# A four-layer decoder trunk: compute order fixed by a clock of TensorE's work, q and k projected transposed, mixer and output projection in one stretch

## The chip, the core and the metric

The kernel runs as one program on one core of a Trainium2 chip. A core has TensorE (PE, matrix multiply), VectorE (DVE), ScalarE (ACT), GpSimd (POOL) and SyncE (SP, which here issues the DMAs). The metric is the device time of one execution in microseconds (us); lower is better. Three runs of the kernel before gave a median of 1271.38 us (1270.69 to 1271.77).

## The reference

Four layers over 256 tokens of 1024 features. Layer i uses mixer i mod 3, so the order is A, B, C, A. All is float32.

```python
for i in range(DEPTH):                      # DEPTH = 4
    kind, j = i % N_MIXERS, i // N_MIXERS
    if kind == 0:   h = mixer_a(...)        # window 128, 16 query heads, 4 key/value heads, sinks, biases
    elif kind == 1: h = mixer_b(...)        # 3 groups of q, k, v (dilation 1, 4, 16), merged by softmax sums
    else:           h = mixer_c(...)        # with 256 tokens: plain causal attention, 16 heads
    x = layer_norm(DN_ALPHA * x + h, ln_g[i, 0], ln_b[i, 0])
    x = layer_norm(DN_ALPHA * x + swiglu(x, w_gate_up[i], w_down[i]), ln_g[i, 1], ln_b[i, 1])
```

In each mixer q and k are projected (x @ w), then rotated on the first 16 of a head's 64 features: pairs (f, f+8) turn by an angle that depends on the token. Scores, softmax, values and an output projection follow. A, B and C have 3, 18 and 6 chunks of projection weights, and two chunks of output weights each; a chunk is 1024 x 512 weights.

## The kernel before

Every float32 product is made of three float16 products (`mm3`, L130 to L132): a weight chunk is scaled by 256 and split into `whi` and `wlo`, the activations into `xth` and `xtl`, and hi x hi, hi x lo and lo x hi are summed in PSUM. `load_w` brings a chunk in two DMAs of 1 MB into `raw`; ACT makes `whi` (L91) and DVE makes `wlo` (L92), 1024 columns at a time, four such pieces a chunk. `wlo` reads `raw` and `whi`, both in SBUF. Four chunks fit in the pool.

A projection (`proj`) takes 128 tokens as the stationary side and a chunk's 512 columns as the moving side, so q and k come out with tokens on the partitions. The bias (mixer A: DVE, L477) or the scaling (ACT, L543 for B and C) brings them to SBUF as `qkv`, POOL rotates them in four small operations (`rope`, L197 to L200, 64 or 128 columns), PE transposes four blocks of 128 x 128 (L206), and `split` writes `qkh` (ACT, L135) and `qkl` (DVE, L137). In mixer A, k is also copied twice over for its four query heads (L488).

`attend` writes out, for each item (a token tile and one or two pairs of heads): scores (L256), masked minimum on DVE (L266), exponential on ACT (L271), transposes of the weights (`flip`, L285), `ph` and `pl` (ACT, DVE), values into `pv` (L130 to L132), division (L309, L311), transposes of the output (L324), `oth` and `otl`. `weave` mixes these steps evenly with the projection steps of the next heads; the last heads are woven with the output projection in `finish`. This source order is only a priority: the framework's scheduler then orders each engine by its own estimate of readiness.

`layer_norm` adds the residual (L349), takes statistics (L351, L353), the root on POOL (L355) and scales (L358, L360, each with two SBUF inputs); then x is transposed (L160) for the next stage. In mixer A the output bias is added to x by DVE (L520, L522). The SwiGLU stage (`ffn`) projects with the weights as the stationary side and 256 tokens moving (128 for its first three chunks), then projects down.

At the start x comes first over SP, then the weights; PE begins with transposes of x.

Of the kernel before, what the change touches and what calls it, by code (L numbers as in the profile page):

```python
# [18 lines left out]
P = 128  # L19
# [24 lines left out]
def trunk(ctx, tc, a, out):  # L44
    nc = tc.nc
    pool = lambda name, bufs, **kw: ctx.enter_context(tc.tile_pool(name=name, bufs=bufs, **kw))
# [14 lines left out]
    cc = const.tile([P, NT, ROT], F32, name="cc")  # L61
    ss = const.tile([P, NT, ROT], F32, name="ss")
    h8 = ROT // 2
# [3 lines left out]
    X = []  # L67
    for t in range(NT):
        xt = const.tile([P, D], F32, name=f"x{t}")
        for h in range(2):  # L70
            nc.sync.dma_start(xt[:, h * 512:h * 512 + 512], a["x"][t * P:(t + 1) * P, h * 512:h * 512 + 512])
        X.append(xt)

# [3 lines left out]
    LAG, LF, LV, LO = 8, 1, 2, 3  # L77
    tok = lambda t: slice(t * P, (t + 1) * P)

    def load_w(src, n=8, piece=2048):  # L80

        hi = w_p.tile([P, 4096], F16, name="whi")
        lo = w_p.tile([P, 4096], F16, name="wlo")
        for c in range(0, n * 512, piece):
            m = min(piece, n * 512 - c)
            s = slice(c, c + m)
            r = raw_p.tile([P, 2048], F32, name="raw")
            nc.sync.dma_start(r[:, :m], src[:, s])
            for d in range(0, m, 1024):
                e = min(d + 1024, m)  # L90
                nc.scalar.activation(hi[:, c + d:c + e], r[:, d:e], AF.Copy, scale=WS)  # L91
                nc.vector.scalar_tensor_tensor(lo[:, c + d:c + e], r[:, d:e], WS, hi[:, c + d:c + e],  # L92
                                               op0=OP.mult, op1=OP.subtract)
        return (hi.rearrange("p (k n) -> p k n", n=512), lo.rearrange("p (k n) -> p k n", n=512))

    def weight_list():
        for li in range(DEPTH):
            kind, j = li % 3, li // 3
            if kind == 0:
                for c in (2, 0, 1):  # L100
                    yield a["w_a"][j, c], 8
# [14 lines left out]
    loaded = []  # L116

    def prefetch(n=1, piece=2048):
        for _ in range(n):
            loaded.append(load_w(*next(weights), piece))  # L120

    def next_w():
        if not loaded:
            prefetch()
        return loaded.pop(0)

    def mm3(ps, st, mv, start, stop):
# [4 lines left out]
        nc.tensor.matmul(ps, st[1], mv[0], start=False, stop=stop)  # L132

# [6 lines left out]

    def sl2(pair, *idx):
        return tuple(p.__getitem__(idx) for p in pair)

    def weave(main, fill):

        nf = 0
# [227 lines left out]
    def new_ps():  # L374
        return {}
# [366 lines left out]
```

## Time and profile before

| | us |
|---|---|
| median of three runs | 1271.38 |
| the profiled execution, whole | 1270.83 |
| its span, first to last instruction | 1268.3 |
| PE busy | 1238.2 |
| DVE busy | 868.7 |
| ACT busy | 657.4 |
| POOL busy | 126.2 |

The profiled execution stands within the three runs, 0.55 us under their median; 2.5 us of it lie outside the span. The granted clock of TensorE was 0.998 over the span. A matmul's record in the trace is longer than the distance to the next one, because matmuls overlap in the pipeline; so PE's busy time hides short waits, and what PE must do at least is read from the distance between the starts of neighbours.

### The profile page before, as it was taken

Reading aid. Unit: us, or ns where it says so; the run is one execution under the profiler, and the core shown is the slowest. Engines: PE = TensorE matmul, PEld = TensorE weight load, DVE = VectorE, ACT = ScalarE, POOL = GpSimd, SP = SyncE. Lnnn points to the kernel's source line nnn. Section 1 sums busy time; section 2 is a strip of 40 time slices with the busy share of each in tenths; the row PEclk is TensorE's granted clock in tenths of the full one; section 3 lists DMA queues with packets and bytes.
Section 4 is the critical chain, followed back from the end, with each engine's and each line's share of the span. In section 5 each row is a group of like instructions: output and inputs, shape, how many; then the busy total and the mean of one; then the engine's idle time right before and its main releaser. Section 6 shows DMA issues by size and latency. Waiting matters only on the chain. (4 is left out here: it accounts for less than half of the span.)

```text
span 1268.3 us, 24652 instructions
## 1 busy us (share of the span) xinstructions
PE 1238.2 (98%) x10352; PEld 829.0 (65%) x10352; DVE 868.7 (68%) x1431; ACT 657.4 (52%) x1097; POOL 126.2 (10%) x262
## 2 busy tenths in 40 slices
PE   7989999999999999999999999999999999999997
PEld 3549988445455555599884445599884445898843
DVE  5997766576576666777665766777665788776652
ACT  5855654345565655556543456556543465465430
POOL 2510000012121112000000110200000041000000
PEclk9999999999999999999999999999999999999999
DMA  8545755655444345147556564247555652475520
GB/s 322 175 164 200 267 201 185 218 206 216 167 163 170 133 147 186 67 168 266 199 183 207 208 217 149 100 167 267 199 183 206 230 186 101 168 266 200 182 84 34
DMA packets 35662, 233.30 MB, mean 184 GB/s; under 512 B 4448, under 2 KB 4448, under 8 KB 9696
## 3 DMA queue, kind: packets, MB, share of 16 engines
q1 hardware_dynamic: 35552, 231.74, 51.8%
q8 instruction: 81, 1.33, 0.4%
q14 instruction: 29, 0.24, 0.1%
HBM read 230.68 MB, written 1.05 MB: 183 GB/s over the span
## 5 line engine op out<-in xcount | busy, mean ns | idle before, releaser
L92 DVE SCALAR_TENSOR_TENSOR wlo<-raw,whi 128x1024 f16<-128x1024 f32 x416 | 501.4, 1225 | 207.2 <-ACT whi L91 206.6
L91 ACT ACTIVATE whi<-raw 128x1024 f16<-128x1024 f32 x416 | 414.5, 1049 | 260.0 <-PE acc L131 89.1
L131 PE MATMUL acc<-xtl,whi 128*128 128x256 f16 (+1 forms) x1792 | 408.2, 250 | 0.0
L132 PE MATMUL acc<-xth,wlo 128*128 128x256 f16 (+1 forms) x1792 | 408.2, 250 | 0.0
L130 PE MATMUL acc<-xth,whi 128*128 128x256 f16 (+1 forms) x1792 | 408.0, 250 | 0.0
L130 PE MATMUL acc<-whi,xth 128*128 128x512 f16 x480 | 183.3, 382 | 2.5 <-ACT xth L135 2.5
L130 PEld LDWEIGHTS <-whi 128*128 128x128 f16 x1792 | 175.3, 98 | 12.0
L131 PEld LDWEIGHTS <-whi 128*128 128x128 f16 x1792 | 175.3, 98 | 11.9
L131 PE MATMUL acc<-wlo,xth 128*128 128x512 f16 x480 | 183.0, 381 | 0.2 <-DVE wlo L92 0.2
L132 PE MATMUL acc<-whi,xtl 128*128 128x512 f16 x480 | 182.8, 381 | 0.3
L132 PEld LDWEIGHTS <-wlo 128*128 128x128 f16 x1792 | 175.3, 98 | 11.7
L130 PE MATMUL acc<-whi,hth 128*128 128x512 f16 x352 | 133.4, 379 | 0.0
L131 PE MATMUL acc<-wlo,hth 128*128 128x512 f16 x352 | 133.4, 379 | 0.0
L132 PE MATMUL acc<-whi,htl 128*128 128x512 f16 x352 | 133.4, 379 | 0.0
L355 POOL TENSOR_TENSOR mv<-mv,nhalf 128x1 f32<-128x1 f32 x16 | 15.8, 988 | 817.2 <-DVE mv L354 817.2
L132 PEld LDWEIGHTS <-xtl 128*128 128x128 f16 x480 | 47.1, 98 | 58.2 <-DVE xtl L137 3.0
L271 ACT ACTIVATE s<-s,mn 128x257 f32<-128x257 f32 (+5 forms) x128 | 66.8, 525 | 33.3 <-DVE mn L266 33.3
L130 PEld LDWEIGHTS <-xth 128*128 128x128 f16 x480 | 47.2, 98 | 48.9 <-issue 4.6
L135 ACT ACTIVATE hth<-hf 128x256 f16<-128x256 f32 x88 | 36.5, 415 | 73.7 <-DVE hf L399 73.7
L131 PEld LDWEIGHTS <-xth 128*128 128x128 f16 x480 | 47.2, 98 | 41.6 <-issue 0.8
L132 PEld LDWEIGHTS <-htl 128*128 128x128 f16 x352 | 34.4, 98 | 41.5
L131 PEld LDWEIGHTS <-hth 128*128 128x128 f16 x352 | 34.4, 98 | 40.8
(92 smaller groups left out, 1427.7 us busy)
## 6 DMA issues: line engine op xcount, KB each, us to landing
raw<-in_w_gu SPq DMA_DIRECT2D x88, 1024.0 KB, 5.0
raw<-in_w_dn SPq DMA_DIRECT2D x40, 1024.0 KB, 4.9
raw<-in_w_b SPq DMA_DIRECT2D x36, 1024.0 KB, 5.0
raw<-in_w_c SPq DMA_DIRECT2D x12, 1024.0 KB, 5.1
raw<-in_w_a SPq DMA_DIRECT2D x10, 1024.0 KB, 5.5
raw<-in_w_ao SPq DMA_DIRECT2D x8, 1024.0 KB, 5.5
gb<-in_ln_g SPq DMA_DIRECT2D x8, 512.0 KB, 4.7
gb<-in_ln_b SPq DMA_DIRECT2D x8, 512.0 KB, 6.2
```

What stands on the lines that cost most here:

```text
L91: nc.scalar.activation(hi[:, c + d:c + e], r[:, d:e], AF.Copy, scale=WS)
L92: nc.vector.scalar_tensor_tensor(lo[:, c + d:c + e], r[:, d:e], WS, hi[:, c + d:c + e], op0=OP.mult, op1=OP.subtract)
L130: nc.tensor.matmul(ps, st[0], mv[0], start=start, stop=False)
L131: nc.tensor.matmul(ps, st[0], mv[1], start=False, stop=False)
L132: nc.tensor.matmul(ps, st[1], mv[0], start=False, stop=stop)
L135: nc.scalar.activation(hi, src, AF.Copy, scale=1.0 if scale is None else scale)
L271: nc.scalar.activation(s[hh][:, pi], s[hh][:, pi], AF.Exp, bias=m[h], scale=-1.0, accum_out=q["l"][:, lc:lc + 1])
L355: nc.gpsimd.tensor_tensor(mv[:, 3:4], mv[:, 2:3], nhalf, op=OP.pow)
```

## The change

The scheduler no longer orders PE, ACT, DVE and POOL: they run what the source says, as it says it (`manual_schedule`). SP keeps its own order. The source sets the order by a clock that adds up the modelled time of PE's work (`spend`, called by each `mm3` and transpose). Work for other engines that should come later is put down with a delay on this clock (`later`): `wlo` 1.2 us after `whi`, rotation 1.0 us after the projection's last matmul and its split 8.5 us after it. A piece of a weight chunk is fed every 2.2 us of the clock (3.2 us in the last layer's mixer). An `Attention` object gives its steps when they are due on the clock (`FLIP`, `VAL`, `OUT` us after the step before), and `drive` interleaves them with the dense steps, which now run on into the output projection: a mixer after its first chunks is one stretch.

q and k are projected with the weights as the stationary side (`proj_t`), so they come out transposed and PE does not transpose them (176 transposes gone). The tokens are the moving side, 256 of them, or 128 in the first chunks of layers 1 to 3. The rotation swaps feature rows with a DVE shuffle over partitions and then does three POOL operations over all rows and 512 columns (256 for layer 0's k and layer 3's k). The split reads SBUF, where it read PSUM. In mixer A the heads are reordered by the host so that k is not doubled, biases of q and k are added by ACT, and the output bias is prepared by ACT and added by POOL (L714, L716).

At the start, x and the first chunk alternate on SP, three small loads go over POOL's queue, twelve matmuls on zeros (`spin`) stand between the first transposes, and k and v of layer 0 go together through the chunk (`products`). The last layer norm scales half by half.

```diff
+    ctx.enter_context(tc.manual_schedule(engines={... "PE", "Activation", "DVE", "Pool"}))
+    FLIP, VAL, OUT, USE, BANK = 4.0, 2.6, 1.6, 1.6, 2.6
+    clock, due, feeding = [0.0], [], {"at": 0.0, "every": 2.2}
+    def later(dt, fn, key=None):
+        due.append((clock[0] + dt, len(due), fn, key))
+        due.sort(key=lambda e: e[0])
+    def spend(us):
+        clock[0] += us
+        while due and due[0][0] <= clock[0]:
+            due.pop(0)[2]()
+        if clock[0] >= feeding["at"]:
+            feed()
+    def parts(hi, lo, r):
+        nc.scalar.activation(hi, r, AF.Copy, scale=WS)
+        later(1.2, lambda: nc.vector.scalar_tensor_tensor(lo, r, WS, hi, op0=OP.mult, op1=OP.subtract), "w")
     def mm3(ps, st, mv, start, stop):
...
+        spend(3 * (mv[0].shape[-1] / 2400 + 0.0025))
-    def weave(main, fill):
...
+    def drive(att, dense, part=1.0):
+        n, total, i = len(dense) * part, att.total, 0
+        burst = 0
+        while i < len(dense) or att.done < total:
+            behind = att.done < total and att.done * n < i * total
+            if (behind or i == len(dense)) and burst < 2 and att.step():
+                burst += 1
+                continue
+            burst = 0
+            pump()
+            if i < len(dense):
+                fn, when = dense[i]
+                if when is None or when() <= clock[0]:
+                    fn()
+                    i += 1
+                    continue
+            if not att.step():
+                spend(0.2)
+    def proj_t(XT, w, js, ts, evac, per=2):
...
+                mm3(cell["ps"][:, j - js[0]], sl2(w, ALL, k, slice(j * P, (j + 1) * P)), sl2(XT, ALL, k, ts),
+                    k == 0, k == NK - 1)
-    def rope(y, t, nh):
...
-        e.tensor_tensor(t1, y[:, :, :ROT], cb, op=OP.mult)
-        e.tensor_tensor(t2[:, :, :h8], y[:, :, h8:ROT], sb0, op=OP.mult)
-        e.tensor_tensor(t2[:, :, h8:], y[:, :, :h8], sb1, op=OP.mult)
-        e.tensor_tensor(y[:, :, :ROT], t1, t2, op=OP.add)
-    def transpose_qk(y, t, dst):
-        ps = ats.tile([P, 4, P], F32, name="at")
-        for j in range(4):
-            nc.tensor.transpose(ps[:, j], y[:, j * P:(j + 1) * P], ident)
-        split(dst[0][:, :, tok(t)], dst[1][:, :, tok(t)], ps)
+    def rope_t(ps, dst, ts, key, bias=None):
...
+        def turn():
+            nc.vector.stream_shuffle(z.rearrange("p j n -> p (j n)"), y.rearrange("p j n -> p (j n)"), swap)
+            nc.gpsimd.tensor_tensor(z, z, table(ss), op=OP.mult)
+            nc.gpsimd.tensor_tensor(y, y, table(cc), op=OP.mult)
+            nc.gpsimd.tensor_tensor(y, y, z, op=OP.add)
+        def store():
+            split(dst[0], dst[1], y)
+            ready[key] = clock[0] + USE
+        ready[key] = 1e9
+        later(1.0, turn, key)
+        later(8.5, store, key)
+            later(2.2, lambda: scale(0), "ln")
+            later(3.5, lambda: scale(1), "ln")
+        def bias_out():
+            nc.scalar.activation(bo, bo, AF.Copy, scale=1.0 / ALPHA)
+            for t in range(NT):
+                nc.gpsimd.tensor_tensor(X[t], X[t], bo, op=OP.add)
+    def spin(n):
+        ps = bank()[0]
+        for _ in range(n):
+            nc.tensor.matmul(ps, idle[:, :P], idle, start=True, stop=True)
```

On PE at the start of the program, the kernel before goes from the transposes of x straight to the first projection (`x_92` and `x_95` are the two token tiles):

```order
L160 MATMUL at<-ident,x_92 128x128 x8
L160 MATMUL at<-ident,x_95 128x128 x8
L130 LDWEIGHTS xth
L130 MATMUL acc<-whi,xth 128x512
L131 LDWEIGHTS xth
L131 MATMUL acc<-wlo,xth 128x512
```

After the change, on PE at the same place (`ph` is a tile of zeros, `x_97` the second token tile):

```order
L827 MATMUL at<-ph 128x512
L213 MATMUL at<-ident,x_97 128x128 x4
L827 LDWEIGHTS ph
L827 MATMUL at<-ph 128x512
L827 LDWEIGHTS ph
L827 MATMUL at<-ph 128x512
L207 LDWEIGHTS whi
L207 MATMUL acc<-xth,whi 128x256
L208 LDWEIGHTS whi
L208 MATMUL acc<-xtl,whi 128x256
```

The second half of x is now transposed after the first two of eight feature blocks, matmuls on zeros stand ahead of the first projection, and the weights are the side that is loaded.

On DVE in the middle of layer 1 (mixer B), the kernel before (`pl` is a flipped weight's low part, `s` and `mn` the masked scores and their minimum):

```order
L137 TENSOR_TENSOR qkl_4410<-at,qkh_4409 128x4x128
L92 SCALAR_TENSOR_TENSOR wlo<-raw,whi 128x1024
L266 ISA s,mn<-at,masks,mn 128x256
L266 ISA mn 128x1
L266 ISA s,mn<-at,masks,mn 128x256
L266 ISA mn 128x1
L92 SCALAR_TENSOR_TENSOR wlo<-raw,whi 128x1024 x3
L137 TENSOR_TENSOR qkl_4410<-at,qkh_4409 128x4x128
```

And after the change, on DVE in the same layer:

```order
L130 SCALAR_TENSOR_TENSOR wlo<-raw,whi 128x1024
L219 TENSOR_TENSOR pl<-at,ph 128x512
L316 STREAM_SHUFFLE qkz<-qkv 128x512
L219 TENSOR_TENSOR qkl_3446<-qkv,qkh_3445 128x512
L130 SCALAR_TENSOR_TENSOR wlo<-raw,whi 128x1024
L219 TENSOR_TENSOR pl<-at,ph 128x512
```

The pieces of weights stand one by one between the attention's operations, a shuffle is new for each half chunk of q and k, and the low part of q and k reads `qkv` in SBUF instead of `at` in PSUM.

On POOL in layer 1, one rotation of the kernel before:

```order
L197 TENSOR_TENSOR rope_3348<-qkv,cc 128x128
L198 TENSOR_TENSOR rope_3349<-qkv,ss 128x8x8
L199 TENSOR_TENSOR rope_3349<-qkv,ss 128x8x8
L200 TENSOR_TENSOR qkv<-rope_3348,rope_3349 128x8x16
L197 TENSOR_TENSOR rope_3402<-qkv,cc 128x128
```

And after the change:

```order
L317 TENSOR_TENSOR qkz<-qkz,ss 128x512
L318 TENSOR_TENSOR qkv<-qkv,cc 128x512
L319 TENSOR_TENSOR qkv<-qkv,qkz 128x512
L317 TENSOR_TENSOR qkz<-qkz,ss 128x512
L318 TENSOR_TENSOR qkv<-qkv,cc 128x512
```

Four operations of 64 or 128 columns have become three of 512, once for each half chunk of 256 tokens.

## Rows read from the trace of the kernel before

**Rows 1.** The page's first part: busy time, share and instructions of each engine.

```profile
PE 1238.2 (98%) x10352; PEld 829.0 (65%) x10352; DVE 868.7 (68%) x1431; ACT 657.4 (52%) x1097; POOL 126.2 (10%) x262
```

**Rows 2.** Groups by line and shape on PE: count | busy us, mean ns | idle before.

```profile
L206 PE MATMUL at<-ident,qkv 128*128 128x128 f32 x176 | 27.4, 274 | 2.7 <-POOL qkv L200 1.6 <-ACT qkv L488 1.0
```

**Rows 3.** Instructions in time on PE: start us, duration us; the distance of starts counts.

```profile
17.05 0.38 PE L130 MATMUL acc<-whi,xth 128*128 128x512 f16 x1
...
17.27 0.38 PE L131 MATMUL acc<-wlo,xth 128*128 128x512 f16 x1
...
1096.40 0.22 PE L130 MATMUL acc<-xth,whi 128*128 128x128 f16 x1
...
1096.57 0.22 PE L130 MATMUL acc<-xth,whi 128*128 128x128 f16 x1
```

**Rows 4.** Busy time by stretch; the first is one of SwiGLU with 256 columns moving.

```profile
core 0: us, PE busy (x) PEld busy (x) DVE busy (x) ACT busy (x) POOL busy (x), PEclk, DMA share, GB/s
130.00:200.00 70.00, 70.00 (x663) 62.97 (x661) 48.65 (x70) 38.98 (x57) 0.00 (x0) 1.00 0.63 225
```

**Rows 5.** The chain that ended last: start us, us, eight transposes in a row.

```profile
1097.57 0.88 PE at L160 x8
```

**Rows 6.** Busy time by stage: mixer 0, SwiGLU 0, mixers 1, 2 and 3, the end.

```profile
0.00:103.00 103.00, 89.54 (x664) 49.86 (x665) 83.67 (x185) 66.84 (x140) 27.04 (x63) 0.98 0.60 212
103.00:272.50 169.50, 169.50 (x1551) 130.39 (x1549) 111.29 (x152) 80.08 (x112) 1.98 (x2) 1.00 0.60 212
272.50:549.00 276.50, 274.54 (x2043) 150.65 (x2042) 188.78 (x308) 160.48 (x261) 47.80 (x99) 1.00 0.45 157
...
718.50:834.00 115.50, 112.92 (x818) 61.38 (x817) 83.80 (x173) 68.65 (x143) 20.06 (x42) 1.00 0.44 155
...
1003.50:1091.00 87.50, 83.03 (x667) 46.87 (x666) 74.46 (x166) 52.57 (x124) 22.45 (x50) 1.00 0.41 148
...
1260.60:1268.30 7.70, 0.11 (x1) 0.00 (x0) 4.39 (x8) 0.00 (x0) 0.99 (x1) 0.85 0.18 68
```

**Rows 7.** Instructions in time at the start: start us, us, engine [idle before, what ended it].

```profile
8.83 1.06 ACT L91 ACTIVATE whi<-raw 128x1024 f16<-128x1024 f32 x1 [6.81 <-DMA raw<-in_w_a]
...
10.42 0.61 PE L130 MATMUL acc<-whi,xth 128*128 128x512 f16 x1 [2.49 <-ACT xth L135]
...
16.16 0.63 PE L130 MATMUL acc<-whi,xth 128*128 128x512 f16 x1
...
16.59 0.42 PE L131 MATMUL acc<-wlo,xth 128*128 128x512 f16 x1
```

**Rows 8.** Groups by line and shape on DVE: count | busy us, mean ns | idle before.

```profile
L92 DVE SCALAR_TENSOR_TENSOR wlo<-raw,whi 128x1024 f16<-128x1024 f32 x416 | 501.4, 1225 | 207.2 <-ACT whi L91 206.6
...
L137 DVE TENSOR_TENSOR qkl<-at,qkh 128x512 f16<-128x512 f32 x44 | 30.1, 685 | 28.1 <-ACT qkh L135 27.8
...
L477 DVE SCALAR_TENSOR_TENSOR qkv<-acc,hth 128x512 f32<-128x512 f32 x12 | 8.2, 682 | 0.6 <-PE acc L132 0.5
```

**Rows 9.** Instructions in time, POOL and DVE in layer 1: start us, us.

```profile
299.23 0.46 POOL L200 TENSOR_TENSOR qkv<-rope,rope 128x128 f32<-128x128 f32 x1
...
299.33 1.43 DVE L92 SCALAR_TENSOR_TENSOR wlo<-raw,whi 128x1024 f16<-128x1024 f32 x1 [0.25 <-ACT whi L91]
...
347.38 0.32 POOL L199 TENSOR_TENSOR rope<-qkv,ss 128x64 f32<-128x64 f32 x1
...
347.59 1.23 DVE L92 SCALAR_TENSOR_TENSOR wlo<-raw,whi 128x1024 f16<-128x1024 f32 x1 [0.74 <-ACT whi L91]
...
347.78 1.35 POOL L200 TENSOR_TENSOR qkv<-rope,rope 128x128 f32<-128x128 f32 x1
...
348.73 1.48 DVE L92 SCALAR_TENSOR_TENSOR wlo<-raw,whi 128x1024 f16<-128x1024 f32 x1
```

**Rows 10.** Instructions in time at the end, DVE and POOL.

```profile
1262.67 0.99 POOL L355 TENSOR_TENSOR mv<-mv,nhalf 128x1 f32<-128x1 f32 x1 [8.08 <-DVE mv L354]
1263.83 1.41 DVE L360 SCALAR_TENSOR_TENSOR x<-x,mv,gb 128x512 f32<-128x512 f32 x2
```

More of the change, by code (lines that the diff above doesn't have):

```diff
@@ new lines, in flush, with pump, go @@
+    def flush(keys):
+        hit = [e for e in due if e[3] in keys]
+        due[:] = [e for e in due if e[3] not in keys]
+        for e in hit:
+            e[2]()
+    side = []
+    def pump(t=None):
+        while side and (side[0][0] <= clock[0] or any(e[1] == t for e in side)):
+            side.pop(0)[2]()
+    def go(steps):
+        for f in steps:
+            pump()
+            f()
+    def parts(hi, lo, r):
+        nc.scalar.activation(hi, r, AF.Copy, scale=WS)
+        later(1.2, lambda: nc.vector.scalar_tensor_tensor(lo, r, WS, hi, op0=OP.mult, op1=OP.subtract), "w")
@@ L94, in load_w, with new_w, feed @@
-        return (hi.rearrange("p (k n) -> p k n", n=512), lo.rearrange("p (k n) -> p k n", n=512))
+                parts(chunk[0][:, c + d:c + d + 1024], chunk[1][:, c + d:c + d + 1024], r[:, d:d + 1024])
+                yield
+    def new_w():
+        ring["alive"] += 1
+        assert ring["alive"] <= 4
+        return [w_p.tile([P, 4096], F16, name=n) for n in ("whi", "wlo")]
+    ring = {"alive": 0, "now": None}
+    loaded = []
+    def feed():
+        if ring["now"] is None:
+            if ring["alive"] == 4:
+                return False
+            src = next(weights, None)
+            if src is None:
+                return False
+            chunk = new_w()
+            loaded.append(chunk)
+            ring["now"] = pieces(src[0], src[1], chunk)
+        if next(ring["now"], 0) == 0:
+            ring["now"] = None
+            return feed()
+        feeding["at"] = clock[0] + feeding["every"]
+        return True
@@ new lines, in next_w, with done @@
+    def next_w():
+        while not loaded or (len(loaded) == 1 and ring["now"] is not None):
+            now = ring["now"]
+            if not loaded or now is None:
+                assert feed()
+                continue
+            if next(now, 0) == 0:
+                ring["now"] = None
+        if any(e[3] == "w" for e in due):
+            flush(["w"])
+        return tuple(p.rearrange("p (k n) -> p k n", n=512) for p in loaded.pop(0))
+    def done(n=1):
+        ring["alive"] -= n
@@ L165, in new_xt, with proj @@
         return (big.tile([P, NK, SEQ], F16, name="xth"), big.tile([P, NK, SEQ], F16, name="xtl"))
[L167 to L174 removed]
+    def proj(XT, w, t, evac, cols=slice(0, 512)):
         cell = {}
@@ L464, in mixer_a, with finish, o, step @@
-    def mixer_a(li, j, XT):
-        bias = hbuf("hth")[:, :1536]
-        bo = hbuf("htl")[:, :D]
+    def finish(li, att, dense, oT, part):
+        PS, w = new_ps(), []
+        cell, load, half, ln = layer_norm(2 * li)
+        def o(t):
+            steps = []
+            for k in range(NK):
+                for h in range(2):
+                    def step(k=k, h=h):
+                        if not w:
+                            w.extend([next_w(), next_w()])
+                        out_steps(PS, oT, NK, w[h], h, t, [k])[0]()
+                    steps.append((step, lambda k=k: att.collected.get((t, k // 2), 1e9)))
+            return steps
+        steps = [(f, None) for f in dense] + [(load, None)]
+        for t in range(NT):
+            steps += o(t) + [(lambda t=t: ln(t, PS), None)]
+        drive(att, steps, part)
+        done(2)
+        return cell
```

623 lines of the change are left out of this document (356 added, 267 removed).

## The prediction

> **What bounds the kernel now.** I read the page's busy times first: PE is busy 98% of the span, every other engine 68% or less [rows 1]. So the question is what PE does and when it has nothing to do. The busy time by stage answers the second half [rows 6]: a SwiGLU stage is full to the last tenth (169.5 of 169.5 us), and it comes four times; PE is idle by 13.5 us in mixer 0, 2.0, 2.6 and 4.5 us in mixers 1 to 3, and for the last 7.6 us.
>
> That idle time is a lower bound, since a matmul's record is longer than its place in the pipeline. The starts of neighbours stand 0.22 us apart at 512 columns and 0.17 us for three matmuls at 128 [rows 3], so 0.216 and 0.056 each. In a stretch of SwiGLU 663 matmuls, some 40 of them with 128 columns, fill 70 us [rows 4]: 0.109 for 256 columns. Eight transposes take 0.88 us [rows 5]: 0.109 each. Counting each mixer's matmuls by form at these distances gives PE work of 77.5, 271.1, 109.4 and 77.9 us in stages of 103.0, 276.5, 115.5 and 87.5 us. What is not work is 25.5, 5.4, 6.1 and 9.6 us; with the end, 54.3 us in all. The rest, 1214 us, can't fall by any order.
>
> Who holds PE in the mixers? DVE is busy 83.7 of 103.0 and 74.5 of 87.5 us in the two A mixers, against 188.8 of 276.5 and 83.8 of 115.5 in B and C [rows 6]. So B and C are bound by PE with small waits, and A is close to bound by DVE. [...]
>
> **The change part by part.** The base is the profiled execution, 1270.83 us, of which 1268.3 are span; the median of the runs is 0.55 us higher.
>
> *Transposes.* 176 of them go [rows 2]: 24 in each A mixer, 96 in B, 32 in C. At 0.109 us: 2.6, 10.5, 3.5 and 2.6 us, 19.2 in all.
>
> *Narrower matmuls.* A chunk of q and k is 48 matmuls of 512 columns (10.35 us), then 96 of 256 (10.48) or 192 of 128 (10.71). Mixer 0 has three chunks at 256: +0.4. B has ten at 256 and two at 128: +2.0. C has three and one: +0.75; mixer 3 about the same, +0.75. Sum +3.9. That the weights now are loaded for 256 or 128 columns does not slow PE: SwiGLU does just that, and the 0.109 and 0.056 are from there.
>
> So PE's work becomes 75.3, 262.6, 106.65 and 76.05 us.
>
> *DVE.* Each half chunk of q and k adds a shuffle of 512 columns. No row shows a shuffle; from below it is bounded by nothing, from above by the conversion of twice the columns, 1.22 [rows 8]. I take 0.6, the 0.685 of a 512-column operation [rows 8] less its overlap with the next. B has 24 (14 us), C 8 (5 us), an A mixer four and two half ones (3 us). The A mixers lose six bias operations of 0.68 (L477, [rows 8]) and the output bias (three operations, some 3.1 us at the width of `wlo`), and gain two small biases of v: net −2.8 with the shuffles. Work on ACT grows by those biases only; it is at 52% [rows 1].
>
> [...] A rotation was four operations of 64 and 128 columns; it is three of 512. Clean ones take 0.32 (64) and 0.46 (128) [rows 9]: 2.2 ns a column, so 1.30 us for 512. B has 72, C 24, an A mixer 12 and six half ones, plus two of 1024 (2.4 each) for the bias. POOL itself has room. But the rows show that it and `wlo` exclude each other: `wlo` takes 1.23 us clean, 1.43 when a POOL operation is 0.1 us ahead, and at 347.78 POOL's operation, 0.46 long when clean, takes 1.35, to just after the end of the `wlo` that was running; the next `wlo` then takes 1.48 [rows 9]. [...]
>
> [...] In B `wlo` (some 80 pieces of 1.2 us) and the low parts of q and k, which now have two SBUF inputs too, take 110 of 276 us, so I take 0.4 of POOL's time: 0.5 us an operation. DVE then has 189 + 14 + 36 = 239 us in B, 101 in C, 82 in mixer 3 and 91 in mixer 0. That is under PE's time in B and C, by little, and over it in the A mixers.
>
> *Order.* The scheduler's order becomes a fixed one, with 4.0 us of PE work between scores and flips, 2.6 to the values. A late operation now holds up all that is queued behind it on its engine: a low part of q and k that waits for POOL holds the masked minima and `wlo` behind it on DVE, and with them the flips on PE. A wait of the trace can go only where a chain on DVE and ACT fits the delay; the clock knows nothing of DVE's load.
>
> Stage by stage. **B:** 262.6 of work, and waits of 4.4 (5.4 before: fixed distances help, a DVE at 90% harms): 267, −9.5. **C:** 106.65 and 3.9 of waits (6.1 before): 110.5, −5. **Mixer 3:** DVE 82 and 3 of its own waits: 85, −2.5. **Mixer 0:** the lower clock level until 16.59 us costs some 3 us before, and the matmuls on zeros run instead of idling; the first chunk can start before 10.42, since half of x and a first piece of weights come first. But the next chunk's `wlo` stand on DVE behind the angle tables, and DVE's 91 us plus about 8 us without input make 99: −4, with the ends at −15 (PE's work and a start of 13) and +11 (all of POOL's time added). **SwiGLU:** 0; a piece every 2.2 us is four in 8.8 us, and a chunk lasts 10.4. **End:** before, both first scalings (L358) ran while POOL made the root (0.99 us), both second ones from 1263.83 [rows 10]; now a first scaling stands behind a second: +0.7.
>
> Sum: 1270.8 − 4 − 9.5 − 5 − 2.5 + 0.7 = 1250.5, so **1250**.
>
> **The rivals.**
>
> *The order fits.* DVE finds room for POOL between its operations, and waits shrink to a microsecond or so in B and C: B 264, C 108, mixer 3 79, mixer 0 92. That is −12.5 − 7.5 − 8.5 − 11 + 0.7: 1232. For it: B and C hold only 5 to 6 us of waits now. Against it: DVE is nearly full in the A mixers.
>
> *The waits only move.* The fixed order gains nothing over the scheduler's; PE waits for the rotation and the low parts as it waited for transposes. Then only PE's work in B and C is saved (8.5 + 2.75), A stays with DVE and loses 2: 1270.8 − 11.25 + 2 + 0.7 = 1262.
>
> *The port decides (slower).* Let s be the share of POOL's time that DVE loses. DVE needs 203 + 94s us in B, 88.6 + 31s in C, 75 + 25s in mixer 3 and 89 + 25s in mixer 0 (own waits included). Up to s = 0.65 B and C stay with PE. At s = 0.72 B's 271, C's 111, 93 and 107 add up to no gain. At s = 0.8 they are 278, 113.5, 95 and 109: 1.5 − 2 + 7.5 + 6 + 0.7, so 1284; at s = 1 it would pass 1310. [...]
>
> *The matmuls don't get shorter overall:* excluded, as the counts and distances above are of the same forms.
>
> **How the numbers follow.** The forecast (1241 to 1258) has 0.44, the fitting order (below 1241) 0.20, moved waits (1258 to 1270) 0.20, the port (above 1270) 0.16. The range runs from 1228, below the fitting order's 1232 by the 4 us that mixer 0's better end has over its 92, to 1270, where moved waits end; it leaves out the port's 0.16 and some 0.03 below. This kernel's measurement tells 0.2% (2.5 us) from no change. Faster by more than that (below 1268.8): 0.44 + 0.20 + 0.14 of the moved waits, 0.78. Within 0.2%: the other 0.05 of the moved waits that are not slower and 0.02 of the port's, 0.07. Slower: 0.14 of the port's and 0.01 of the moved waits, 0.15.
>
> **What would show it.** Right: PE work in mixer 1 down to 262.6 us with the stage near 267; no L206; POOL operations of 512 columns at 1.3 us when clean; DVE about 240 us busy in mixer 1, with `wlo` longer than 1.23 on average. The fitting order: mixers 1 and 2 within 2 us of PE's work. Moved waits: PE's list of waits names the minima, `ph`, `pl` or `qkl` with as many microseconds as not-work now. The port: `wlo` at 1.6 us or more, DVE over 95% in mixer 1, PE waiting for `wlo`. Wrong from the start: first projection not before 10.4 us, or the SwiGLU stages over 169.5 us.

## The result: slower by a tenth, and the profile after

| kernel | median us (range) | ratio to before, 95% interval | profiled execution us | its span us | PE's work us | span less work us |
|---|---|---|---|---|---|---|
| before | 1271.04 (1269.04 to 1271.77) | | 1270.83 | 1268.3 | 1214.0 | 54.3 |
| after | 1395.66 (1392.06 to 1396.37) | 1.098 (1.0955 to 1.100) | 1396.37 | 1394.6 | 1198.7 | 195.9 |

1250 was forecast, with 1228 to 1270 as the range. PE's work is counted as in the prediction: every matmul by its form, at the distance at which its neighbours start in a full stretch. It fell by the 15.3 us that were forecast. What is not work was 54.3 us and is now 195.9: all of the loss is time in which PE waits, or runs at a lower granted clock (0.78 over mixer 0, before 0.98). By stage, less the work forecast for each, mixer 0 holds 65.9 us of it (23.7 forecast), B 33.7 (4.4), C 32.4 (3.9) and mixer 3 54.5 (9.0).

The first part of the page of after, which answers [rows 1], then PE's and the clock's line of its second part (40 slices of the span, in tenths):

```profile
PE 1264.8 (91%) x11676; PEld 946.0 (68%) x11676; DVE 974.1 (70%) x1502; ACT 671.6 (48%) x1117; POOL 269.0 (19%) x225
...
PE   7667999999999998879999997989999967799997
...
PEclk8768999999999999999999999999999976899999
```

No engine is full, and PE less so than before (91% against 98%). Where that happens, the busy times by stage tell; these are mixer 0, SwiGLU 0, mixers 1, 2 and 3 and the end, in the columns of [rows 6]:

```profile
0.00:141.20 141.20, 99.54 (x766) 68.04 (x767) 102.86 (x194) 72.29 (x148) 45.14 (x63) 0.78 0.47 163
141.20:310.00 168.80, 168.75 (x1555) 131.07 (x1553) 103.63 (x139) 76.88 (x106) 1.46 (x1) 0.99 0.56 191
310.00:606.30 296.30, 270.72 (x2694) 199.88 (x2695) 249.41 (x366) 164.97 (x264) 133.58 (x75) 0.99 0.48 158
775.00:914.00 139.00, 117.53 (x1061) 81.00 (x1060) 112.93 (x202) 73.42 (x148) 43.76 (x27) 0.95 0.46 154
1082.50:1213.00 130.50, 98.22 (x921) 71.50 (x922) 95.64 (x186) 60.94 (x141) 40.19 (x55) 0.82 0.37 124
1386.00:1394.60 8.60, 0.03 (x1) 0.00 (x0) 4.57 (x8) 0.00 (x0) 0.99 (x1) 0.79 0.17 62
```

SwiGLU is as full as it was. The mixers are longer: 141.2 us instead of 103.0, 296.3 instead of 276.5, 139.0 instead of 115.5, 130.5 instead of 87.5. In none of them is DVE full (73 to 84%), and in the two A mixers PE and DVE each stand idle for about a quarter of the time or more. That is how it looks when engines wait for each other in turn.

What PE waited for (engine, line, what it waited for, by whom: us in total, times, longest us), the top of the list of before and then of after. In after, L213 is every transpose, L207 to L209 are the three products of `mm3`, L523 is the second scaling of a layer norm, L471 the division, L219 every low part and L433 the exponential:

```profile
PE at L160 <- DMA x<-in_x: 3.9, 2, 3.6
PE at L324 <- DVE oy L311: 3.4, 2, 2.5
```

```profile
PE at L213 <- DVE x L523: 38.8, 17, 6.8
PE at L213 <- DVE oy L471: 17.4, 9, 4.5
PE pv L207 <- DVE oy L471: 14.0, 7, 3.6
PE pv L209 <- DVE pl L219: 11.6, 7, 5.1
PE at L213 <- ACT s L433: 7.1, 4, 4.6
```

**Wait one: the transposes of x.** At the end of mixer 0, first DVE, then PE, in time (start us, us, [idle before, what ended it]):

```profile
133.04 0.15 DVE L516 TENSOR_SCALAR mv<-mv 128x1 f32<-128x1 f32 x1
133.12 4.63 DVE L130 SCALAR_TENSOR_TENSOR wlo<-raw,whi 128x1024 f16<-128x1024 f32 x4
137.67 0.75 DVE L521 SCALAR_TENSOR_TENSOR x<-x,mv,gb 128x512 f32<-128x512 f32 x1
138.53 0.75 DVE L523 SCALAR_TENSOR_TENSOR x<-x,mv,gb 128x512 f32<-128x512 f32 x1
...
139.43 1.09 PE L213 MATMUL at<-ident,x 128*128 128x128 f32 x4 [6.78 <-DVE x L523]
```

The stage that begins fetches its weights first (`early = [next_w() ...]`), which puts four `wlo` on DVE ahead of the scaling of x tile 1; and the transposes of that tile are due 1.9 us of PE's work after the scaling was *issued*, so they stand in PE's queue ahead of matmuls that could run. PE stops for 6.78 us.

**Wait two: an attention item's low part.** The same in the middle of mixer 0, POOL and DVE and then PE:

```profile
63.36 5.62 POOL L716 TENSOR_TENSOR x<-x,htl 128x1024 f32<-128x1024 f32 x2
...
63.92 2.86 DVE L130 SCALAR_TENSOR_TENSOR wlo<-raw,whi 128x1024 f16<-128x1024 f32 x1 [3.51 <-ACT whi L129]
66.70 2.83 DVE L219 TENSOR_TENSOR qkl<-qkv,qkh 128x512 f16<-128x512 f32 x1
69.45 1.21 DVE L130 SCALAR_TENSOR_TENSOR wlo<-raw,whi 128x1024 f16<-128x1024 f32 x1
70.59 1.28 DVE L219 TENSOR_TENSOR pl<-at,ph 128x512 f16<-128x512 f32 x2
...
71.32 0.23 PE L209 MATMUL pv<-qkh,pl 128*128 128x64 f16 x1 [5.15 <-DVE pl L219]
```

`pl` stands behind a `wlo` and a `qkl` that each take over twice their clean time while POOL adds the output bias: 2.86 us against the 1.21 of the next `wlo`, and 2.83 against a mean of 0.68 in rotation_all_dve, a run below with nothing as long on POOL. The clock allots 2.6 us from flips to values. Worked out from the trace for each of the eight items of mixer 0, the time from the end of the flips to the end of `pl` had a median of 2.3 us and a maximum of 10.3 (before: 2.6 and 3.1). Two items are late, 10.3 and 9.3 us, and both meet this one addition; the other six take 2.6 at most. The delay suits the median, and PE pays for the maximum.

**The clock beside the idle time.** Busy time by stretch of mixer 0 in after; the number behind POOL's is the granted clock:

```profile
52.00:60.00 8.00, 2.88 (x38) 1.93 (x36) 8.00 (x19) 4.47 (x12) 7.92 (x12) 0.77 0.61 206
60.00:72.00 12.00, 4.88 (x33) 2.55 (x34) 8.49 (x10) 7.26 (x18) 11.34 (x13) 0.50 0.34 116
72.00:83.00 11.00, 8.43 (x48) 5.78 (x48) 10.08 (x28) 9.02 (x24) 1.31 (x4) 0.50 0.30 95
```

PE was busy for 2.9 of 8 us, and its clock then read 0.50 for 23 us, the last 11 of them with 8.4 us of matmuls. Counted from the traces over the four mixers, neighbours that start about twice as far apart as in a full stretch cost some 30 us (before: some 7). If the waits bring the lower clock, which their order in time suggests and no run isolates, part of the waiting is paid a second time.

**The port.** This is the author's name for what [rows 9] show: some operations of POOL and of DVE that run at the same time lengthen each other. What the two engines share there, no run shows. Two groups of DVE and two of POOL in after (count | busy us, mean ns | idle before); they answer [rows 8]:

```profile
L130 DVE SCALAR_TENSOR_TENSOR wlo<-raw,whi 128x1024 f16<-128x1024 f32 x412 | 540.2, 1336 | 58.3 <-ACT whi L129 56.4
L316 DVE STREAM_SHUFFLE qkz<-qkv 128x512 f32<-128x512 f32 x40 | 29.1, 729 | 0.0
...
L318 POOL TENSOR_TENSOR qkv<-qkv,cc 128x512 f32<-128x512 f32 x40 | 74.3, 1859 | 0.0
L319 POOL TENSOR_TENSOR qkv<-qkv,qkz 128x512 f32<-128x512 f32 x40 | 72.9, 1822 | 3.1
```

A POOL operation of 512 columns takes 1.27 us at its shortest (forecast: 1.30) and 1.8 on average; `wlo` went from 1.225 to 1.336.

### The profile page after: what moved, and what is told of

Read it like the earlier page. It is cut to its first block, busy times and chain, and to the rows that moved or that the text cites. A ratio compares the mean times of both kernels' runs of the same rounds, so it can differ in the third digit from the quotient of the medians.

```text
span 1394.6 us, 27266 instructions
## 1 busy us (share of the span) xinstructions
PE 1264.8 (91%) x11676; PEld 946.0 (68%) x11676; DVE 974.1 (70%) x1502; ACT 671.6 (48%) x1117; POOL 269.0 (19%) x225
## 5 line engine op out<-in xcount | busy, mean ns | idle before, releaser
L207 PE MATMUL acc<-xth,whi 128*128 128x256 f16 (+1 forms) x2608 | 610.1, 254 | 2.8 <-ACT qkv L312 2.8
L209 PE MATMUL acc<-xth,wlo 128*128 128x256 f16 (+1 forms) x2608 | 609.9, 254 | 2.7 <-DVE wlo L130 2.6
L208 PE MATMUL acc<-xtl,whi 128*128 128x256 f16 (+1 forms) x2608 | 610.1, 254 | 0.3 <-DVE xtl L219 0.3
L130 DVE SCALAR_TENSOR_TENSOR wlo<-raw,whi 128x1024 f16<-128x1024 f32 x412 | 540.2, 1336 | 58.3 <-ACT whi L129 56.4
L207 PEld LDWEIGHTS <-whi 128*128 128x128 f16 x2608 | 258.8, 99 | 23.4 <-issue 3.0
L209 PEld LDWEIGHTS <-wlo 128*128 128x128 f16 x2608 | 258.6, 99 | 23.2 <-DVE wlo L130 4.0
L208 PEld LDWEIGHTS <-whi 128*128 128x128 f16 x2608 | 258.7, 99 | 22.2 <-issue 2.5
L207 PE MATMUL acc<-whi,hth 128*128 128x512 f16 x352 | 133.4, 379 | 0.0
L209 PE MATMUL acc<-whi,htl 128*128 128x512 f16 x352 | 133.4, 379 | 0.0
L317 POOL TENSOR_TENSOR qkz<-qkz,ss 128x512 f32<-128x512 f32 (+1 forms) x44 | 68.5, 1557 | 196.1 <-DVE qkz L316 195.8
L433 ACT ACTIVATE s<-s,mn 128x257 f32<-128x257 f32 (+5 forms) x128 | 67.0, 525 | 80.6 <-DVE mn L428 72.0
L318 POOL TENSOR_TENSOR qkv<-qkv,cc 128x512 f32<-128x512 f32 (+1 forms) x44 | 80.2, 1822 | 0.0
L319 POOL TENSOR_TENSOR qkv<-qkv,qkz 128x512 f32<-128x512 f32 (+1 forms) x44 | 77.0, 1749 | 3.4
L219 DVE TENSOR_TENSOR qkl<-qkv,qkh 128x512 f16<-128x512 f32 (+1 forms) x48 | 52.9, 1103 | 25.0 <-ACT qkh L217 24.8
L209 PEld LDWEIGHTS <-htl 128*128 128x128 f16 x352 | 34.4, 98 | 41.5
```

The source lines that it names most:

```text
L130: later(1.2, lambda: nc.vector.scalar_tensor_tensor(lo, r, WS, hi, op0=OP.mult, op1=OP.subtract), "w")
L207: nc.tensor.matmul(ps, st[0], mv[0], start=start, stop=False)
L208: nc.tensor.matmul(ps, st[0], mv[1], start=False, stop=False)
L219: nc.vector.tensor_tensor(lo, src, hi, op=OP.subtract)
L317: nc.gpsimd.tensor_tensor(z, z, table(ss), op=OP.mult)
L318: nc.gpsimd.tensor_tensor(y, y, table(cc), op=OP.mult)
```

## The experiments

Two theories stood at the beginning. *Port*: the wide rotation on POOL takes time from DVE's operations. *Order*: the fixed order puts operations into the queues of PE and DVE ahead of others that could run. All times are medians of four or eight executions, beside 1270.6 to 1271.2 for before. The stage lengths below run from the ninth gate product of one SwiGLU to the last of it and on to the ninth of the next, so that every mixer includes its borders; the SwiGLU part between is 70.0 us by the scheduler's order and 68.1 by the fixed one.

### First round: take the scheduler back, narrow the rotation, delay x, widen before

```
after_scheduler:       - ctx.enter_context(tc.manual_schedule(engines={...}))
after_narrow_rotation: - nc.gpsimd.tensor_tensor(z, z, table(ss), op=OP.mult)      (and the other two)
                       + nc.gpsimd.tensor_tensor(z[:, :, :n // 8], z[:, :, :n // 8], tab8(ss), op=OP.mult)
after_late_x:          - side.append((clock[0] + 1.9, t, ...
                       + side.append((clock[0] + (1.9 if t == 0 else 9.0), t, ...
before_wide_rotation:  - four operations of 64 and 128 columns a rotation
                       + e.tensor_tensor(w, yf, tb, op=OP.mult); e.tensor_tensor(w, w, tb, op=OP.mult)
                       + e.tensor_tensor(yf, yf, w, op=OP.add)                     (512 columns each)
```

> The changed kernel without its fixed order: the framework's scheduler orders PE, ACT, DVE and POOL again; transposed projections, wide rotation on POOL and everything else stay. Theory 'port' (POOL's 512-column operations and wlo exclude each other, and that alone makes DVE late): the port is as busy as before, so most of the loss stays, over 1340 us. Theory 'order' (instructions that wait hold up what stands behind them on PE and DVE): PE does other work while DVE is late, so it falls to 1255 to 1290 us.

> The changed kernel with the fixed order, but each POOL operation of the rotation works on an eighth of its columns (64 instead of 512); the rest of q and k stays unrotated, which is left out. Theory 'port': POOL's time in the rotations falls from 226 us to under 50, wlo goes back to 1.23 us, and the time falls by 60 us or more, to under 1335. Theory 'order': PE still waits for layer norms and divisions, and the time falls by less than 40 us, to over 1355.

> The changed kernel, but the transposes of x of the second token tile after a layer norm are due 9.0 us of PE's clock after the scaling is put down, instead of 1.9; nothing else moves by more than these transposes do. Theory 'order': the 38.8 us that PE waits at these transposes go, and with them some of the stretches at the lower clock level: 1340 to 1360 us. Theory 'port': the wait only moves to the next thing that needs DVE, less than 15 us gained, over 1380 us.

> The kernel before, but its rotation is replaced by three POOL operations over all 512 columns (256 for mixer A's k), as many and as wide as in the changed kernel; they multiply and add without rotating, which is left out. Theory 'port': 30 us or more slower than before, over 1300 us, most of it in the A mixers, with wlo at 1.33 us or more. Theory 'order': the scheduler finds other work meanwhile, less than 15 us slower, under 1286 us.

| run | us | ratio (95%) | mixer 0 | B | C | mixer 3 | end |
|---|---|---|---|---|---|---|---|
| before | 1271 | | 149.8 | 375.3 | 215.4 | 187.0 | 60.9 |
| after | 1395.7 | 1.098 | 190.3 | 396.7 | 239.5 | 231.1 | 64.6 |
| after_scheduler | 1368.7 | 1.077 (1.075 to 1.079) | 174.0 | 421.7 | 229.8 | 201.8 | 61.2 |
| after_narrow_rotation | 1363.6 | 1.073 (1.071 to 1.074) | 185.4 | 385.2 | 233.0 | 222.0 | 64.5 |
| after_late_x | 1350.9 | 1.063 (1.061 to 1.065) | 178.8 | 387.3 | 226.6 | 219.9 | 64.5 |
| before_wide_rotation | 1312.1 | 1.032 (1.030 to 1.035) | 155.7 | 397.7 | 222.0 | 195.0 | 60.8 |

One line of diff, the due time of one tile's transposes, is worth 45 us: PE's wait for x went from 38.8 to 5.4, with less time at a lower granted clock on top (from 100 to 120 us it read 0.86 instead of 0.76). In the list of after_late_x:

```profile
PE at L213 <- DVE oy L471: 17.0, 8, 3.8
...
PE at L213 <- DVE x L523: 5.4, 7, 1.3
```

Narrowing the rotation is worth 32 us in after, and the wide one costs 41 in the otherwise unchanged kernel before, over half of it in B. There PE's first wait is the one that the prediction's port rival left out, because it isn't DVE's: the transposes of q and k wait for POOL itself.

```profile
PE at L205 <- POOL qkv L199: 17.5, 15, 3.1
```

The narrow rotation also gives the port's price. The first part of its page:

```profile
PE 1252.1 (92%) x11676; PEld 939.4 (69%) x11676; DVE 916.8 (67%) x1502; ACT 671.0 (49%) x1117; POOL 131.8 (10%) x225
```

DVE's busy time fell by 974.1 − 916.8 = 57.3 us for 269.0 − 131.8 = 137.2 us less on POOL, a share of 0.42.

Neither theory won the round. By time alone, after_scheduler (over 1340) and before_wide_rotation (over 1300) came out as *port* had it, after_narrow_rotation (over 1355) and after_late_x (1340 to 1360) as *order* had it. But *port* put most of the wide rotation's loss into the A mixers, and it was in B; and in after_scheduler the A mixers got shorter by 16 and 29 us and B longer by 25, which neither theory had foreseen.

### Second round: do they add, and what is left?

```
after_late_x_narrow:       both edits above
after_late_x_long_delays:  - FLIP, VAL, OUT, USE, BANK = 4.0, 2.6, 1.6, 1.6, 2.6
                           + FLIP, VAL, OUT, USE, BANK = 7.0, 5.0, 3.5, 3.0, 4.0     (with late x)
after_ln_scaling_first:    + flush(["ln"])
                             early = [next_w() for _ in range(EARLY)]                (and in the mixers)
after_late_x_no_rotation:  - the shuffle and the three POOL operations               (with late x)
```

> The kernel after with both edits tried singly so far: the transposes of the second x tile due 9.0 us of TensorE's work after the scaling instead of 1.9, and the three POOL operations of each rotation on one eighth of the columns (the rest of q and k stays unrotated). Two causes that add up: 1395.7 - 45 - 32 = 1319 (1312 to 1326). If one wait had merely covered the other, so that each cure already gave most of both: 1332 to 1348. Either way some 50 us over the kernel before would be left, which neither names.

> Late transposes of x as before, and all five delays of the clock lengthened: scores to flips 4.0 to 7.0 us of TensorE's work, flips to values 2.6 to 5.0, values to outputs 1.6 to 3.5, use of a stored part 1.6 to 3.0, reuse of a bank 2.6 to 4.0. If the clock's delays are too short for DVE's queue (the theory): the waits of PE for oy, pl, s and ph, 56 us together in the run with late x, fall by a third or more, and the time by 15 to 30, to 1320 to 1336. If DVE is short of time in these stages (the rival), longer delays only move the waits: 1343 to 1358. If the longer delays leave too little dense work beside the last attention of a mixer, it gets slower: above 1358.

> The kernel after with one change of order: the four scaling operations of the second x tile are issued ahead of the weight pieces that a stage fetches at its start, four times in the program (mixer to SwiGLU of each layer); the transposes stay due after 1.9 us. If the pieces of wlo in front of them on DVE make x late (4 x 1.16 us = 4.6 us at each of four places): the waits of PE for x fall from 38.8 to about 20 us and the time by 18 to 26, to 1370 to 1378. If x is late whatever stands before it, because mean and root are late: 1388 or more.

> Late transposes of x, and the shuffle and all three POOL operations of every rotation left out (q and k stay unrotated); delays and order of everything else as they were. If what is left over the kernel before comes from the rotation (its chain of shuffle, three operations and the store, and the port): 1285 or less. If it comes from the fixed order, whose in-order queues on DVE hold up the attention: 1300 to 1320, with the waits of PE for oy, pl and s still above 30 us.

| run | us | ratio (95%) |
|---|---|---|
| after_late_x_narrow | 1320.5 | 1.039 (1.037 to 1.041) |
| after_late_x_long_delays | 1334.2 | 1.050 (1.048 to 1.052) |
| after_ln_scaling_first | 1380.0 | 1.086 (1.084 to 1.089) |
| after_late_x_no_rotation | 1314.8 | 1.035 (1.033 to 1.036) |

Narrow rotation and late x add up (1319 expected). The four `wlo` ahead of the scaling account for 16 of the 45 us of x: PE's wait for x fell to 22.6, near the 20 expected, and the time by a little less than the 18 to 26 expected. In the list of after_ln_scaling_first:

```profile
PE at L213 <- DVE x L523: 22.6, 17, 2.5
```

Longer delays gave 17, within what was expected, but PE's waits for `oy`, `pl`, `s` and `ph` fell only from 57 to 47 us and not by the third that was expected with it; one wait for `s` alone is 13.9. And without any rotation 44 us are still missing, nearly all in the A mixers: mixer 0 175.1, B 371.2, C 219.3, mixer 3 209.3. That is the fixed order or the new structure of the code.

### Third round: what holds the A mixers?

```
no_rotation_no_output_bias: - nc.gpsimd.tensor_tensor(X[t], X[t], bo, op=OP.add)
no_rotation_v_first:        - dense = [q1 ...] + [done] + tail + [bias_out]
                            + dense = tail + [q1 ...] + [done] + [bias_out]
no_rotation_scheduler:      - ctx.enter_context(tc.manual_schedule(engines={...}))
before_bias_on_pool:        - three DVE operations on bo and X
                            + nc.scalar.activation(bo, bo, AF.Copy, scale=1.0 / ALPHA)
                            + nc.gpsimd.tensor_tensor(X[t], X[t], bo, op=OP.add)     (twice)
```

> The run with late transposes of x and no rotation (1314.8), with one thing more left out: the two POOL operations of 1024 columns per A mixer that add the output bias to x. By stage that run lost 25.3 us in mixer 0 and 22.3 in mixer 3 against the kernel before, and next to nothing in B and C together. If these two operations (2.8 us each, while DVE's wlo and qkl wait behind them and pl behind those) are what holds PE in mixer 0, its stage falls by 6 to 12 us, mixer 3's by 2 to 8: 1296 to 1306. If the delay only moves to the next link of the chain: 1311 or more.

> The run with late transposes of x and no rotation (1314.8), with v of mixer 3 projected ahead of the second q chunk instead of behind it. There the low parts are ready a median of 4.1 and at most 15 us ahead of the values that use them, because v isn't. If that holds back mixer 3 (two items of the attention at a time, and nothing dense left when v comes): its stage falls by 6 to 14 us, 1301 to 1309, and the other stages stay. If the attention only fills the same gaps elsewhere: 1311 to 1317.

> The run with late transposes of x and no rotation (1314.8), with the scheduler's order on the compute engines instead of the fixed one. With rotation and early transposes the scheduler had mixers 0 and 3 shorter by 16 and 29 us than the fixed order, and B longer by 25. If the fixed order is what is left in the A mixers, they fall by 12 or more each here too, while B may rise. If the code's own structure (one stretch with the output) is it, they stay within 6 us. For the whole: 1280 to 1300 by the first, 1310 to 1335 by the second.

> The kernel before with one part of the change alone: the output bias of the A mixers scaled on ACT and added to x by two POOL operations of 1024 columns, instead of three DVE operations (0.71 and two of 1.22, 3.15 us per A mixer). If DVE's time bounds the A mixers, as the prediction had it: 1264 to 1268, 3 us per mixer. If the POOL operations hold DVE's port as long as they run (2.4 to 2.8 us each): 1270 to 1278. If the scheduler finds cover for either: 1269 to 1272.

| run | us | ratio (95%) | mixer 0 | B | C | mixer 3 | end |
|---|---|---|---|---|---|---|---|
| after_late_x_no_rotation | 1314.8 | 1.035 (1.033 to 1.036) | 175.1 | 371.2 | 219.3 | 209.3 | 64.7 |
| no_rotation_no_output_bias | 1309.9 | 1.030 (1.029 to 1.032) | 172.1 | 371.2 | 219.3 | 208.8 | 64.5 |
| no_rotation_v_first | 1310.2 | 1.031 (1.030 to 1.033) | 173.5 | 371.2 | 219.3 | 206.0 | 64.5 |
| no_rotation_scheduler | 1262.0 | 0.993 (0.991 to 0.994) | 154.5 | 366.5 | 211.0 | 188.0 | 61.3 |
| before_bias_on_pool | 1281.5 | 1.008 (1.006 to 1.009) | 155.2 | 375.3 | 215.4 | 193.5 | 60.9 |

The bias and the late v are 5 us each, below the low end of what was expected if they were the cause. The order is 53: with the scheduler's, the same operations take 1262.0, which is less than before and 18 us below the range on record for this case. B is 8.8 us shorter than before there and C 4.4, as much as the saved work of PE (8.5 and 2.75 were forecast) or more. But this run has no rotation at all, and before has its narrow one; what before would gain without it was not run, so that the 9 us are PE's saved work is likely and not shown. So without the rotation the code's structure is not to blame: "a mixer is one stretch with its output" costs little by itself (mixer 0 is 4.7 us longer than before there, mixer 3 1.0).

The bias alone, put on POOL in before, costs 10.7 us, more than any of the three expectations. The rows show what all three had left out, POOL's own queue (POOL, then DVE, in mixer 0); that it makes up the whole price is not shown:

```profile
37.75 0.45 POOL L200 TENSOR_TENSOR qkv<-rope,rope 128x128 f32<-128x128 f32 x1
38.16 6.63 POOL L522 TENSOR_TENSOR x<-x,htl 128x1024 f32<-128x1024 f32 x2
44.75 1.45 POOL L197 TENSOR_TENSOR rope<-qkv,cc 128x128 f32<-128x128 f32 x1
```

```profile
40.52 2.06 DVE L92 SCALAR_TENSOR_TENSOR wlo<-raw,whi 128x1024 f16<-128x1024 f32 x1 [0.25 <-ACT whi L91]
42.50 0.34 DVE L266 CUSTOM_DVE_ANT_0 s<-at,masks,nsink 128x128 f32<-128x128 f32 x1
```

A rotation whose input was ready at 38.1 (the end of its bias operation, L477) started at 44.75. `wlo`, with two inputs in SBUF, was held (2.06 us), and the minimum, which reads its scores from PSUM, ran at its usual 0.34 under the same POOL operation. The means of after split in the same way: `qkl`, with both inputs in SBUF, took 1.148 us (0.684 in rotation_all_dve below), `pl`, with one in PSUM, 0.684 (0.681). Whether the place of the inputs decides, no run shows.

### Fourth round: the same two prices under the scheduler, and the rotation on DVE

That left a contradiction. Without rotation the fixed order costs 53, but in after, taking it away gave back only 27. Under the scheduler, rotation and early x together cost 107, not 36 and 45.

```
scheduler_late_x:              after_late_x without manual_schedule
scheduler_early_x_no_rotation: no_rotation_scheduler with clock[0] + 1.9 for both tiles
rotation_mostly_dve:           scheduler_late_x, and
                               - nc.gpsimd.tensor_tensor(y, y, table(cc) ...   + nc.vector. ...  (and y + z, and the bias)
rotation_all_dve:              z * table(ss) on nc.vector too
```

> The scheduler's order, late transposes of x, and the rotation as the change has it. If the rotation costs under the scheduler what it costs under the fixed order (36): 1262 + 36 = 1298 (1290 to 1306), and the early transposes are what cost the run with the scheduler alone its other 70. If the scheduler handles the rotation badly (B 46 us longer than before in that run): 1340 to 1366, and the transposes are worth little there.

> The scheduler's order, early transposes of x as in the change, and no rotation. By the first theory (the early transposes cost 70 under the scheduler): 1325 to 1340. By the second (the rotation does): 1262 to 1280.

> The scheduler's order, late transposes of x, the rotation complete with one operation left on POOL (sine times the shuffled) and two on DVE (cosine times, and the sum), and the output bias added by DVE instead of POOL. Without rotation, and with the bias off POOL (worth up to 10), the time would be some 1252. DVE gets 44 half chunks x 2 x 0.68 = 60 us more; POOL holds the port a third as long. If POOL's length is the price of the rotation: 1265 to 1282, about the kernel before. If it is the rotation's chain, whoever does it, or DVE's time: 1290 to 1320.

> As the run with the rotation mostly on DVE, but all of it there: 44 x 0.68 = 30 us more DVE work, and nothing long on POOL. If the port is the price: below that run, 1258 to 1275, and the version that beats both kernels. If DVE's time is: above it by 10 to 25, with DVE over 90% busy in mixer 1.

| run | us | ratio (95%) | mixer 0 | B | C | mixer 3 | end |
|---|---|---|---|---|---|---|---|
| scheduler_late_x | 1377.8 | 1.085 (1.083 to 1.086) | 171.3 | 422.2 | 235.9 | 205.4 | 61.0 |
| scheduler_early_x_no_rotation | 1267.1 | 0.997 (0.996 to 0.998) | 154.1 | 369.1 | 212.9 | 187.2 | 61.5 |
| rotation_mostly_dve | 1310.2 | 1.032 (1.030 to 1.034) | 164.1 | 389.5 | 222.0 | 196.0 | 61.2 |
| rotation_all_dve | 1287.5 | 1.013 (1.012 to 1.015) | 161.8 | 376.1 | 215.3 | 190.6 | 61.6 |

Without the rotation, early x costs 5 us under the scheduler. With the rotation in place late x doesn't help: 1377.8 is 9 us more than after_scheduler, and above both ranges on record. The rotation on POOL costs 116 there (1377.8 − 1262.0). What ACT and DVE waited for in scheduler_late_x:

```profile
ACT qkh L216 <- POOL qkv L318: 188.7, 43, 9.8
```

```profile
DVE qkl L218 <- ACT qkh L216: 105.2, 36, 4.6
```

The scheduler put the split of q and k into ACT's and DVE's queues long before POOL was done, and the exponentials, `ph`, `pl` and minima stood behind. In after, whose order stores 8.5 us of PE's work later on purpose, the same wait of ACT is 29.8 us. So the fixed order isn't bad as such: it allows for this rotation, and with it (and late x) it is 27 us faster than the scheduler's.

Most of that price is POOL's length: with one operation of three left on POOL (and the bias on DVE, worth some 10 at most) the time falls by 68, with none by 90, though DVE's work grows. But the first lies in the range of the rival, and the second 12 us above its own, so the chain or DVE's time has a part too: with all of it on DVE, ACT still waits 60.9 us for the rotation (`ACT qkh L216 <- DVE qkv L318`). The complete kernel with the rotation on DVE has B and C within 0.8 us of before and is 17 us slower in all (12 of it in mixer 0, 3.6 in mixer 3). No complete version of the change that was run beats the kernel before, and in none does PE's saved work show in B or C.

## Why the prediction was wrong

One path through the runs adds up: 1271 as before, −9 for the change without its rotation and by the scheduler (1262.0), +53 for the fixed order (1314.8), +36 for the rotation (1350.9), +45 for the early transposes of x (1395.7). Each price holds beside the others in this sequence only; the fourth round shows how far they depend on each other. The −9 compares a kernel without rotation with before, which has its own.

- *PE's work: right.* −15.3 us, as forecast, shown in the counts of matmuls by form. It reached the time at most in no_rotation_scheduler.
- *SwiGLU and end: right.* 168.8 against 169.5 us; at the end a second scaling at 1389.02 delays the next first one to 1389.69, as described, for under 1 us.
- *The start: right, but worth nothing visible.* The first projection starts at 10.19 instead of 10.42, and its matmuls stand as close as in a full stretch from 12.0 on instead of 16.6; what mixer 0 gained there it lost many times over later. The lower clock level until 16.59, which the prediction charged with some 3 us, is its author's reading of the distances, and no run shows it: the granted clock of before read 1.00 from 10.4 to 16.6 us, with most starts 0.43 us apart. After the change it read 0.50 from 9 to 11 us and 0.51 from 11 to 12.
- *DVE's sum: too low by 10 to 14 us a mixer, its terms nearly right.* 249, 113, 96 and 103 us in B, C, mixer 3 and mixer 0 against 239, 101, 82 and 91. The longer stages of B, C and mixer 3 take in six or seven more pieces of `wlo` than before, which is most of the excess there; mixer 0 has two fewer, and its excess stays open. The shuffle was 0.73 long against 0.6, POOL's operation 1.27 at its shortest against 1.30, the port's share 0.42 against 0.4. That share was an estimate from the time of `wlo` and the low parts, and no run shows that it follows from this time; the runs showed the 57.3 us of DVE for 137.2 of POOL in its place.
- *The step that failed: from these sums to times.* Each stage was set at the larger of PE's work and DVE's sum, plus a few microseconds of waits: 4.4 in B, 3.9 in C, 3 in mixer 3, some 8 without input in mixer 0. What is not PE's work was 4.4, 3.9, 9.0 and 23.7 us by that, and became 33.7, 32.4, 54.5 and 65.9, while no engine was full in any of these stages. The operations stand in chains (minimum, exponential, flip, `pl`, value, output) that PE waits for in a fixed order, and a late link costs time though its engine has room. So taking seven eighths of the rotation off POOL gave 32 us, with DVE at 70% before it; how much of that is the 57 us by which DVE's busy time fell and how much POOL's own length in the chain is not divided. What stands in a queue behind a late operation should have been weighed: the `pl` behind `wlo` and `qkl` kept PE for 5.15 us, and ACT's waits for POOL came to 188.7 us in scheduler_late_x.
- *The order: named and priced with the wrong sign.* "A late operation now holds up all that is queued behind it" stood in the text, and the sum took one microsecond off B's waits and two off C's. Without the rotation it costs 53 us, 42 of them in the two A mixers with their borders. Under the fixed order, leaving the output bias out or projecting v earlier gave 5 us each; whether the scheduler's order pays for them too was not run, so they can't be counted as parts of the 53. Longer delays gave 17 with the rotation in place; without it they weren't tried. Where the 53 arise stays open: that it is the tail of the chains' times is argued from the trace, not shown by a run. In mixer 0 the longest time from flips to `pl` is 10.0 us in after_late_x_no_rotation and 2.4 in no_rotation_scheduler, which fits; in mixer 3 it is 6.3 and 4.8, and as much time is lost there, so this one link can't be all of it.
- *The transposes of x: not priced at all.* The diff had their due time, 1.9 us, and the weights fetched ahead of the scaling. Neither was set against the row that mattered, four `wlo` of 1.225 us.
- *Lower clock:* the prediction counted on more of the full level at the start, and not on losing it in the middle. By the distances of neighbours some 23 us more than before go there, as part of the prices above.
- *The rivals.* "The waits only move" had the mechanism and put an unfounded ceiling on it: as much waiting as before. It became 3.6 times as much (54.3 to 195.9 us). "The port decides" had the chance of a time above 1270, and the time did come out there, but not by its mechanism: at the measured share of 0.42 its own sums (203 + 94s in B) leave B and C with PE and give no loss. It looked at DVE's share of time (over 95%; it is 84% in B), while POOL's results are late long before DVE is full.

## What to carry to other kernels

An engine's busy time bounds a stage from below only; before an order is fixed, follow each chain through every engine's queue, with the longest time that each link had in the trace and not its median, and ask what stands behind the operation that comes late. An operation moved to an idle slow engine wasn't free here (512 columns took POOL 1.27 us at its shortest, and DVE 0.69 in rotation_all_dve): its results (ACT waited 188.7 us for them in scheduler_late_x), its own queue (a rotation behind the bias started 6.65 us after its input) and the time that it cost DVE (0.42 of POOL's own) all lay on the chain. When several parts of a change are slow together, undo them one at a time and in pairs, since the price of one (the rotation: 36 or 116 us) depends on the others.

## What was unexpected of the hardware

- POOL additions of 1024 columns, estimated at 2.4 us each, took 2.8 in mixer 0 of after (5.62 for two) and 3.3 in that of before_bias_on_pool (6.63), beside `wlo`; the shortest in after took 2.34.
- After 8 us with 2.9 us of matmuls, PE's clock was granted at 0.50 for 23 us, even while matmuls filled 8.4 of the last 11; matmul neighbours then stand 0.21 us apart instead of 0.11 (scores at 62.64 and 62.85).
- A granted clock near 0.50 comes back several times (1140 to 1150 and 1170 to 1180 us, in mixer 3): the whole of mixer 0 reads 0.78 and mixer 3 0.82, where before read 0.98 and 1.00.
